# V by seven block products, block columns built in place without the root, and one scores tile, in a one-core attention and FFN layer

## The chip, the cores and the metric

The kernel runs on one core of a Trainium2 chip. The metric is the device time of one execution in microseconds (us). The profile is one execution, taken by the hardware profiler. Its engines are PE (TensorE; PEld is its weight load), DVE (VectorE), ACT (ScalarE), POOL (GpSimd) and SP (SyncE, which here issues DMAs). On-chip memory is SBUF, and TensorE writes its results to PSUM.

## What is computed

One layer of a streaming encoder for 2048 tokens of 1024 features: chunked attention with 16 heads of 64, and then a dense FFN with a width of 2816. Each is preceded and followed by a root-mean-square norm. Cut to what matters:

```
h = rms_norm(x, g_pre_mix)              # x * rsqrt(mean(x^2) + 1e-6) * gain
q, k, v = split_heads(h @ w_qkv)        # 16 heads of 64
for each chunk c of 64 tokens:          # keys: the chunk and the 8 before it
    sc = q[c] @ k[c-8..c] / 8 + bias(head, distance)
    o[c] = softmax(sc) @ v[c-8..c]
x = x + rms_norm(o @ w_o, g_post_mix)
h = rms_norm(x, g_pre_ffn)
x = x + rms_norm((silu(h @ w_gate) * (h @ w_up)) @ w_down, g_post_ffn)
```

A norm is a gain for each feature and one number, the root, for each token. Features lie on the partitions in the products, so the root of a token is a row that multiplies columns, and it can as well be applied to the result of the product.

## The kernel before

**Products.** Each operand is split into hi and lo parts (ACT rounds hi, DVE subtracts it to get lo), and a product is three matmuls, hi·hi, hi·lo and lo·hi (`products`, L184 to L186). Q and K, and gate and up, use seven block products in place of eight for a 2 x 2 block scheme. Their token-side blocks are called B11, B21, T1, T2, B22, T3, T4 and their weight-side blocks A11, A12, S1, S2, S4, S3, A22. T and S blocks are sums and differences of the others. V uses plain products.

**Stages.** `project` takes two groups of 1024 tokens. For each, `values_of` makes V and `queries_keys` makes Q and K (four blocks c of seven products, each in two halves of 12 matmuls), and `emit_v` and `emit_qk` send them to memory. Then attention goes through four quarters n of 512 tokens, eight head pairs p each, and four blocks ib of 128 queries: 128 slots. In a slot stand, in TensorE's order: the scores of a slot two ahead (`scores`, L484 and L485), some products of the quarter's output projection as filler (`o_quarter`), four transposes for each of two heads (L517), more filler, the transposes of the fifth key block (L528), and at each fourth slot the product with V (`output`). Quarter 0 has no fifth block. After a last output projection the FFN runs as gate/up 0, down 0, gate/up 1, down 1 (`gate_up`, `down`).

**What sets the order.** TensorE runs in the order in which the program is written. The other engines' orders are made by a scheduler from the dependences. Side work (the squares and roots of a norm, building blocks, late writes of the residual) stands in a list `later`; `tick` takes its steps as TensorE's work advances, where 1.0 stands for three 512-column matmuls. Weights come through `Stream`, where two numbers of each item say how many items ahead it is loaded and split: (4, 3) before. `block_items` makes the S blocks with four POOL sums (L810).

**Columns before.** For V, `column` multiplies x by the gain, splits it and sums its squares. For Q and K, x is loaded a second time, `norm` multiplies by gain and root (`Blocks.first`, `second`, `third`), and `emit_qk` splits the result straight from PSUM or from its terms (L425, L426). A root takes a sum over partitions on TensorE into a PSUM tile (`pssq`), a power on POOL (L274), and a spread back over partitions by TensorE (`prs`, L334). The program's name for scores in PSUM is `st`, for exponentials in SBUF `sc`, for transposed ones `pT`.

## Time and profile before

| | us |
|---|---|
| time, median of 3 runs | 2571.29 (2569.76 to 2573.14) |
| the profiled execution's own time | 2576.7 |
| its span, first to last instruction | 2574.6 |
| PE busy | 2405.3 (93%), 11562 matmuls |
| DVE busy | 1715.4 (67%) |
| ACT busy | 1156.4 (45%) |
| POOL busy | 648.8 (25%) |

Busy time says which engine is near its limit on the average. Which wait costs time is read by stage and from the waits: a wait row names the instruction that waited, what released it, the total, the number of waits and the mean. Matmuls are pipelined, so that the distance of their starts is what one costs, and not its own duration. `<-` stands between what is written and what is read, and the matmul rows name the tiles by the program's names.

### The profile page before, as it was taken

Reading aid. Unit: us, or ns where it says so; the run is one execution under the profiler, and the core shown is the slowest. Engines: PE = TensorE matmul, PEld = TensorE weight load, DVE = VectorE, ACT = ScalarE, POOL = GpSimd, SP = SyncE. Lnnn points to the kernel's source line nnn. Section 1 sums busy time; section 2 is a strip of 40 time slices with the busy share of each in tenths; the row PEclk is TensorE's granted clock in tenths of the full one; section 3 lists DMA queues with packets and bytes.
Section 4 is the critical chain, followed back from the end, with each engine's and each line's share of the span. In section 5 each row is a group of like instructions: output and inputs, shape, how many; then the busy total and the mean of one; then the engine's idle time right before and its main releaser. Section 6 shows DMA issues by size and latency. Waiting matters only on the chain. (4 is left out here: it accounts for less than half of the span.)

```text
span 2574.6 us, 33484 instructions
## 1 busy us (share of the span) xinstructions
PE 2405.3 (93%) x11562; PEld 1942.4 (75%) x11562; DVE 1715.4 (67%) x2679; ACT 1156.4 (45%) x2047; POOL 648.8 (25%) x501
## 2 busy tenths in 40 slices
PE   8899889977899899998799999999999989999998
PEld 6788677765677676776677888888878878888887
DVE  7767755636565655667877886676768786565567
ACT  5534443326566555565423333345533323334444
POOL 3232124403333433433332232200013222220002
PEclk8999899988899999999899999999999999999999
DMA  7556789859876887885545433356764643336654
GB/s 257 174 152 192 239 251 252 249 156 222 237 208 177 226 237 201 246 241 169 187 144 192 138 102 111 107 184 219 251 203 135 203 160 110 115 104 230 201 181 159
DMA packets 230648, 484.13 MB, mean 188 GB/s; under 512 B 26416, under 2 KB 42816, under 8 KB 227408
## 3 DMA queue, kind: packets, MB, share of 16 engines
q1 hardware_dynamic: 228368, 470.47, 58.9%
q0 software_dynamic: 2112, 11.54, 2.4%
q8 instruction: 91, 1.49, 0.2%
q14 instruction: 77, 0.63, 0.1%
HBM read 370.18 MB, written 134.79 MB: 196 GB/s over the span
## 5 line engine op out<-in xcount | busy, mean ns | idle before, releaser
L810 POOL TENSOR_TENSOR raw<-raw,raw 128x1024 f32<-128x1024 f32 x120 | 318.8, 2656 | 1001.0 <-DVE w_w_T L131 328.0
L184 PE MATMUL pb<-hb,w_w_T 128*128 128x512 f32 x720 | 287.6, 400 | 33.3 <-DVE terms L890 17.5
L501 POOL TENSOR_SCALAR sc<-sc,rows 128x640 f32<-128x640 f32 (+4 forms) x256 | 193.5, 762 | 382.7 <-DVE rows L500 328.8
L186 PE MATMUL pb<-hb,w_w_T 128*128 128x512 f32 x720 | 285.8, 397 | 0.0
L185 PE MATMUL pb<-hb,w_w_T 128*128 128x512 f32 x720 | 285.6, 397 | 0.0
L497 ACT ACTIVATE sc<-sc,nmax 128x640 f32<-128x640 f32 (+4 forms) x256 | 193.1, 756 | 147.1 <-DVE nmax L493 146.9
L493 DVE CUSTOM_DVE_ANT_0 sc<-st,bias 128x640 f32<-128x640 f32 (+4 forms) x256 | 180.4, 738 | 114.6 <-PE st L485 66.2
L184 PE MATMUL pa<-hb,w_w_B 128*128 128x512 f32 x480 | 189.2, 394 | 5.2 <-ACT terms L871 4.5
L184 PEld LDWEIGHTS pb<-hb,w_w_T 128*128 128x128 f32 x720 | 138.8, 193 | 66.9 <-issue 23.6
L185 PE MATMUL pa<-hb,w_w_B 128*128 128x512 f32 x480 | 188.6, 393 | 0.0
L186 PE MATMUL pa<-hb,w_w_B 128*128 128x512 f32 x480 | 188.2, 392 | 0.0
L484 PE MATMUL st<-k,q 128*128 128x384 f32 (+1 forms) x448 | 146.3, 346 | 38.2 <-DVE nmax L493 24.4
L131 DVE TENSOR_TENSOR w_w_T<-raw,w_w_T 128x1024 fp32r<-128x1024 f32 x120 | 163.4, 1362 | 22.5 <-ACT w_w_T L130 21.9
L131 DVE TENSOR_TENSOR w_w_B<-raw,w_w_B 128x1024 fp32r<-128x1024 f32 x90 | 116.1, 1290 | 89.0 <-ACT w_w_B L130 88.9
L130 ACT ACTIVATE w_w_T<-raw 128x1024 fp32r<-128x1024 f32 x120 | 126.7, 1056 | 98.1 <-PE pa L186 43.7
L185 PEld LDWEIGHTS pb<-hb,w_w_T 128*128 128x128 f32 x720 | 139.1, 193 | 28.9
L186 PEld LDWEIGHTS pb<-hb,w_w_T 128*128 128x128 f32 x720 | 138.4, 192 | 29.6
L130 ACT ACTIVATE w_w_B<-raw 128x1024 fp32r<-128x1024 f32 x90 | 95.2, 1058 | 125.2 <-PE pb L186 82.3
L186 PE MATMUL pd<-a,w_d_T 128*128 128x512 f32 (+1 forms) x368 | 139.9, 380 | 0.1
L184 PE MATMUL pd<-a,w_d_T 128*128 128x512 f32 (+1 forms) x368 | 139.9, 380 | 0.0
L185 PE MATMUL pd<-a,w_d_T 128*128 128x512 f32 (+1 forms) x368 | 139.8, 380 | 0.0
L892 ACT ACTIVATE terms<-terms 128x512 f32<-128x512 f32 x65 | 41.1, 632 | 210.5 <-DVE terms L890 210.5
(212 smaller groups left out, 5874.5 us busy)
## 6 DMA issues: line engine op xcount, KB each, us to landing
raw<-in_w_gu SPq DMA_DIRECT2D x88, 512.0 KB, 4.1
q<-q SPq DMA_DIRECT2D x64, 512.0 KB, 6.6
k<-k SPq DMA_DIRECT2D x56, 512.0 KB, 8.6
raw_d<-d_S SPq DMA_DIRECT2D x88, 256.0 KB, 3.5
raw_a<-aT SPq DMA_DIRECT2D x88, 256.0 KB, 3.8
bias<-ext_d SPq DMA_DIRECT2D x128, 144.0 KB, 8.6
aT<-T SPq DMA_DIRECT2D x66, 256.0 KB, 3.1
raw_d<-in_w_d SPq DMA_DIRECT2D x66, 256.0 KB, 3.8
```

The source lines that it names most:

```text
L130: act.activation(hi, raw, AF.Copy)
L131: dve.tensor_tensor(lo, raw, hi.bitcast(F32), op=ALU.subtract)
L184: pe.matmul(pt, a_hi, b_hi, start=first, stop=False, skip_group_check=go_on)
L185: pe.matmul(pt, a_hi, b_lo, start=False, stop=False, skip_group_check=go_on)
L186: pe.matmul(pt, a_lo, b_hi, start=False, stop=last, skip_group_check=go_on)
L484: pe.matmul(st[:, a:b], q[:, 2 * h, cols], kk[:, h, key], start=True, stop=False)
L493: dve.tensor_tensor_reduce(out=sc[:, :n], in0=st[:, c0 : c0 + n], in1=rev, scale=-1.0, scalar=3.0e38, op0=ALU.add, op1=ALU.min, accum_out= ...
L497: act.activation(sc[:, :n], sc[:, :n], AF.Exp, bias=nmax, scale=-1.0, accum_out=rows[:, 0:1])
L501: last_pool[0] = pool.tensor_scalar(sc[:, :n], sc[:, :n], rows[:, 1:2], 1.0, op0=ALU.mult, op1=ALU.mult)
L810: last_pool[0] = pool.tensor_tensor(r[to], r[a], r[b], op=ALU.add)
L892: act.activation(terms[0], terms[0], AF.Silu)
```

## The change

- V is made by the same seven block products (`values_of` is rewritten, w_v is laid out in blocks); the terms are combined by DVE and POOL, and ACT multiplies by the token's root when V leaves.
- x is loaded once, raw, into the slots of T3 and T4. `build` multiplies it there by the gain (ACT), sums the squares (on POOL now), and makes the blocks in place. No root is applied. In Q and K, `emit_qk` multiplies by the row of roots on the way out, on DVE for the results of block B21 and on POOL for the others, and then splits the product `t`.
- The S blocks are summed in place of their raw blocks, so eight raw buffers in project and six in the FFN do; Q, K, gate and up items are loaded six ahead. V needs S blocks too.
- Scores go to one PSUM tile that is kept (`scores_bank`). Its last 256 columns take the fifth-block transposes, which had PSUM tiles of their own. Head 0's scores are cut after 512 columns, and so lie at 0 to 640, and head 1's at 640 to 1280.
- One reciprocal for both heads of a slot, after both maxima; POOL normalises both after it. The first attention job is loaded during the last block of Q and K, into slots of blocks.
- For the FFN's first group only B11, B21 and T1 are built during the last output projection, and the other four blocks during gate/up 0. Both late writes stand in gate/up 0 with wider steps.

```diff
-    def emit_v(n, m, u, pt, ready_):
...
+    def emit_v(n, m, u, t):
+        act.activation(t, t, AF.Copy, scale=rs[n][:, m : m + 1])
+        sp.dma_start(v_d[n][:, m, u * HALF : u * HALF + HALF], t)
+    def emit_qk(n, p, which, src, eng=dve):
         scale = (0.125, 1.0)[which]
+        t = narrow("t")
+        eng.tensor_tensor(t, src, rows_of[n], op=ALU.mult)
         hi, lo = (narrow(m).bitcast(F32R) for m in ("hi", "lo"))
-        act.activation(hi, src, AF.Copy, scale=scale)
-        dve.scalar_tensor_tensor(lo, src, scale, hi.bitcast(F32), op0=ALU.mult, op1=ALU.subtract)
+        act.activation(hi, t, AF.Copy, scale=scale)
+        dve.scalar_tensor_tensor(lo, t, scale, hi.bitcast(F32), op0=ALU.mult, op1=ALU.subtract)
...
+    def scores_bank():
+        if "S" not in phase:
+            phase["S"] = phase["psa"].tile([P, 3 * HALF], F32, name="st", bufs=1)
+        return phase["S"]
...
-                cuts = [(P, 512, 768), (768, 1024, 1408)]
+                cuts = [(0, 512, 640), (640, 1024, 1280)]
...
-            st = phase["psa"].tile([P, 3 * HALF], F32, tag="S", name="st", bufs=1)
+            st = scores_bank()
...
-                dve.reciprocal(rows[:, 1:2], rows[:, 0:1])
...
+            dve.reciprocal(rows[:, 2:4], rows[:, 0:2])
+            for h in range(2):
+                sc = self.sc[ib, h]
+                last_pool[0] = pool.tensor_scalar(
+                    sc[:, :n], sc[:, :n], rows[:, 2 + h : 3 + h], 1.0, op0=ALU.mult, op1=ALU.mult
...
-                tt = phase["psa"].tile([P, 4, P], F32, tag="tt", name="tt", bufs=2)
+                tt = scores_bank()[:, 1280:1536].rearrange("p (h q) -> p h q", h=2)
                 for h in range(2):
                     pe.transpose(tt[:, h, :], sc[h][:, b * P : b * P + P], ident)
-                act.activation(self.pT[:, :, 4, cols], tt[:, 0:2, :], AF.Copy)
+                act.activation(self.pT[:, :, 4, cols], tt, AF.Copy)
...
-    def v_stream(u, k):
...
+            if n == ("B11" if early else "B21"):
+                sum_("A21", "A21", "A22")
+                sum_("A11", "A11", "A21")
             if n == "B21":
...
+                sum_("A12", "A12", "A11")
+            if n == "T2":
+                sum_("A21", "A11", "A22", ALU.subtract)
             return w
...
-            (lambda n=n: fetch_(at.get(n, ())), lambda _, n=n: make(n), 4, 3) for n in BLOCKS
+            (lambda n=n: fetch_(at.get(n, ())), lambda _, n=n: make(n), *ahead.get(n, (6, 3))) for n in BLOCKS
...
+        def after(name, m, pt):
+            if name == "B11":
+                act.activation(p1[m], pt, AF.Copy)
+            elif name == "B21":
+                put(s0, m, 0, pt, p1[m])
+            elif name == "T1":
+                act.activation(z[m], pt, AF.Copy)
+            elif name == "T2":
+                dve.tensor_tensor(p1[m], p1[m], pt, op=ALU.subtract)
+                pool.tensor_tensor(z[m], z[m], p1[m], op=ALU.add)
+            elif name == "B22":
+                put(s1, m, 0, pt, z[m])
+            elif name == "T3":
+                dve.tensor_tensor(p1[m], pt, p1[m], op=ALU.subtract)
+                put(s1, m, 1, pt, z[m], ALU.subtract)
+            else:
+                put(s0, m, 1, pt, p1[m])
...
             def closing(pts, terms, n, p, op=ALU.subtract):
                 def go(i):
                     dve.tensor_tensor(terms[i], pts[i], terms[i], op=op)
-                    emit_qk(n, p, i, terms[i])
+                    emit_qk(n, p, i, terms[i], pool)
...
+            def prep(t, k, x_):
...
+                add_square(x_, totals[2 * g + t], k == 0, pool)
+                act.activation(x_, x_, AF.Copy, scale=gt[:, PRE_MIX, k : k + 1])
...
+                if g + 1 == NG:
+                    if name == "T1":
+                        jobs[0].load(True)
+                    return
...
+                elif name == "T4":
+                    later.extend(timed(
+                        (12.0, roots(2, 3.0)), (15.0, roots(3, 3.0)),
+                        (20.0, build(1, "B22", 3.0)), (34.0, build(1, "T4", 3.0)), (50.0, build(1, "T3", 2.0)),
+                    ))
```

Line numbers in the profile are those of the kernel before. In the orders of the change: L497 and L498 are the scores, L532 the four transposes, L543 the fifth-block transposes and L544 their copy, L418 the product with the row of roots, L421 the lo split, L1201 the subtraction ahead of it, L816 the weight sums, L252 the square sums, L685 and L686 the block differences on POOL, L276 the power of the root.

The first place is TensorE's order within an attention slot, with the waits. First as it was:

```order
L517 MATMUL tt<-ident,sc 128x128 [waits Activation_49,Pool_49]
L517 MATMUL tt<-ident,sc 128x128 x3
L184 MATMUL mm<-hb_24_4549,w_1_6364 128x512
L185 MATMUL mm<-hb_24_4549,w_1_6364 128x512
L186 MATMUL mm<-hb_24_4549,w_1_6364 128x512
L528 MATMUL tt<-ident,sc 128x128 [waits DVE_49]
L528 MATMUL tt<-ident,sc 128x128
L484 MATMUL st<-k_0_7012,q_0_7009 128x384
L485 MATMUL st<-k_0_7012,q_0_7009 128x384
L484 MATMUL st<-k_0_7012,q_0_7009 128x256
L485 MATMUL st<-k_0_7012,q_0_7009 128x256
```

The same place in the change:

```order
L532 MATMUL tt<-ident,sc 128x128 [waits PE_49,Pool_49]
L532 MATMUL tt<-ident,sc 128x128 x3
L184 MATMUL mm<-hb_21_4255,w_0_5534 128x512
L185 MATMUL mm<-hb_21_4255,w_0_5534 128x512
L186 MATMUL mm<-hb_21_4255,w_0_5534 128x512
L543 MATMUL st<-ident,sc 128x128 [waits DVE_49]
L543 MATMUL st<-ident,sc 128x128
L497 MATMUL st<-k_4_5689,q_4_5688 128x512 [waits Activation_49]
L498 MATMUL st<-k_4_5689,q_4_5688 128x512
L497 MATMUL st<-k_4_5689,q_4_5688 128x128
L498 MATMUL st<-k_4_5689,q_4_5688 128x128
```

The fifth-block transposes now write `st`, and the first matmul of the scores waits for ACT. In all 93 slots of quarters 1 to 3 where that matmul waits so, the ACT instruction is the copy L544 of the transposes just ahead of it. The cut of the scores has moved from 384 to 512 columns.

The second place is VectorE's order in Q and K, around the last two blocks of one c (T3 and T4). First as it was:

```order
L1156 TENSOR_TENSOR terms<-pb,terms 128x512
L426 SCALAR_TENSOR_TENSOR lo<-terms,hi 128x512
L1156 TENSOR_TENSOR terms<-pb,terms 128x512
L131 TENSOR_TENSOR w_w_T_1640<-raw_1595,w_w_T_1640 128x1024
L426 SCALAR_TENSOR_TENSOR lo<-terms,hi 128x512
L1156 TENSOR_TENSOR terms<-pb,terms 128x512
L426 SCALAR_TENSOR_TENSOR lo<-terms,hi 128x512
```

and in the change:

```order
L1201 TENSOR_TENSOR terms<-pb,terms 128x512
L421 SCALAR_TENSOR_TENSOR lo<-t,hi 128x512
L1201 TENSOR_TENSOR terms<-pb,terms 128x512
L131 TENSOR_TENSOR w_w_T_1471<-raw_1308,w_w_T_1471 128x1024
L421 SCALAR_TENSOR_TENSOR lo<-t,hi 128x512
L1201 TENSOR_TENSOR terms<-pb,terms 128x512
L421 SCALAR_TENSOR_TENSOR lo<-t,hi 128x512
```

VectorE's order is the same, but the split now reads `t`, which POOL makes from `terms`.

The third place is POOL's order in the change, behind the last Q and K of the first group, up to the powers that give the second group's roots (L276):

```order
L816 TENSOR_TENSOR raw_1852<-raw_1852,raw_1815 128x1024
L686 TENSOR_TENSOR hb_10_1849<-hb_11_1899,hb_10_1849 128x512 x2
L252 TENSOR_TENSOR total<-total,sq 128x512 x2
L685 TENSOR_TENSOR hb_10_1849<-hb_10_1849,hb_11_1899 128x512
L816 TENSOR_TENSOR raw_1902<-raw_1902,raw_1817 128x1024
L685 TENSOR_TENSOR hb_10_1849<-hb_10_1849,hb_11_1899 128x512
L686 TENSOR_TENSOR hb_10_1849<-hb_11_1899,hb_10_1849 128x512 x2
L276 TENSOR_TENSOR hr<-ms,neg_half 128x4
L816 TENSOR_TENSOR raw_1935<-raw_1815,raw_1937 128x1024
L816 TENSOR_TENSOR raw_1994<-raw_1817,raw_1996 128x1024
L276 TENSOR_TENSOR hr<-ms,neg_half 128x4
```

The roots now stand behind weight sums, square sums and block differences. Before, the same two powers stood behind weight sums alone, the square sums having been made by VectorE.

More of the change, by code (lines that the diff above doesn't have):

```diff
@@ L666, in all, with need @@
+        def need(self, name):
+            while name not in self.done:
+                later.popleft()[1]()
         def all(self, w):
@@ L847, in product @@
         def product(pts, name, first, after):
+            if b.raw:
+                b.need(name)
             hi, lo = back.take()
@@ L1101, in columns @@
-    def columns(w, n, cols, total, eng):
-        c = {}
-        def load(k):
-            c[k] = io("x")
-            sp.dma_start(c[k], x[n][:, k, :])
-        return behind(w, KT, 2, load, lambda k: column(n, k, c.pop(k), total, cols, eng))
-    def values_of(n, cols, between):
-        for u in range(2):
-            pts = [bank("pv") for _ in range(4)]
-            for k in range(KT):
-                hi, lo = front.take()
-                for m in range(4):
-                    c = slice(m * P, m * P + P)
-                    products(pts[m], cols.hi(k, c), cols.lo(k, c), hi, lo, k == 0, k == KT - 1)
-                    yield 3 * C512
-                    if k == KT - 1:
-                        emit_v(n, m, u, pts[m], n in said_rs)
@@ L1201, in project @@
[L1201 to L1219 removed]
+        totals = {}
@@ new lines, in now, with roots, go @@
+        def now(steps):
+            for _, f in steps:
+                f()
+        def roots(n, w):
+            def go():
+                later.extendleft(reversed(scaled(n, totals[n], w)))
+            return [(0.0, go)]
+        front.ahead(-8)
+        now(build(0, "L11 each"))
+        for n in (-7, -6, -5):
+            front.ahead(n)
+        now(build(0, "L21"))
+        front.ahead(-4)
+        now(build(0, "L12"))
+        front.ahead(-3)
+        now(build(0, "L22"))
+        for k, (_, f) in enumerate(build(0, "B11")):
+            f()
+            if k == 0:
+                front.ahead(-2)
@@ L1402, in trunk @@
     drain()
[L1403 removed]
+    later.extend(timed(
+        (0.5, first("T2", 3.0)), (13.0, first("B22", 2.0)), (22.0, first("T4", 2.0)), (31.0, first("T3", 1.0)),
+    ))
     for c in ffn():
```

386 lines of the change are left out of this document (214 added, 172 removed).

## The prediction

> **What bounds the kernel now.** I read the stage table first (busy time of each engine by stretch), then the waits of TensorE, then the timeline of single attention slots. In the rows of the stage table the columns are: stretch, its length in us, busy time of PE, PEld, DVE, ACT and POOL with counts, granted PE clock, DMA share, GB/s. The stretches are, in order: V of the first 1024 tokens, Q and K of them, V and then Q and K of the second, attention of quarter 0, of quarters 1 to 3, the last output projection, gate/up 0, down 0, gate/up 1.
>
> ```profile
> 5.90:121.30 115.40, 99.47 (x408) 79.69 (x409) 90.32 (x116) 62.76 (x107) 37.91 (x21) 0.91 0.63 213
> 121.30:282.10 160.80, 154.58 (x674) 127.58 (x674) 116.61 (x129) 74.80 (x111) 36.48 (x15) 0.98 0.61 184
> 282.10:389.30 107.20, 95.66 (x410) 77.29 (x409) 68.34 (x97) 45.70 (x76) 29.12 (x24) 0.94 0.78 245
> 389.30:559.20 169.90, 159.68 (x673) 129.96 (x671) 94.53 (x100) 55.90 (x78) 60.03 (x49) 0.96 0.78 222
> 572.50:676.00 103.50, 79.37 (x444) 60.48 (x445) 62.86 (x248) 60.73 (x180) 37.47 (x69) 0.87 0.96 233
> 676.00:1190.00 514.00, 480.57 (x3061) 364.35 (x3061) 310.51 (x759) 313.06 (x680) 180.15 (x207) 0.99 0.76 212
> 1190.00:1255.00 65.00, 50.54 (x226) 40.00 (x223) 53.79 (x69) 30.61 (x48) 24.29 (x11) 0.89 0.60 201
> 1255.00:1702.00 447.00, 431.18 (x1876) 355.11 (x1876) 316.89 (x362) 149.91 (x202) 111.94 (x45) 0.98 0.42 135
> 1702.00:1912.00 210.00, 210.00 (x928) 173.93 (x928) 147.15 (x229) 111.02 (x193) 0.21 (x1) 1.00 0.72 235
> 1912.00:2349.00 437.00, 425.69 (x1855) 350.76 (x1854) 308.55 (x347) 141.07 (x185) 114.56 (x44) 0.98 0.44 144
> ```
>
> TensorE is the bound nearly everywhere. In down 0 it is busy all 210.00 us for 928 matmuls, so a 512-column matmul costs 210.00/928 = 0.226 us. At that price V of one group (384 matmuls before) would take 86.9 us, and Q and K (672) 152.1. The stages lose 28.5 us (115.4 - 86.9), 8.7, 20.3 and 17.8 to waits and to a clock that falls after them (0.91, 0.94). Quarters 1 to 3 of attention leave 33 of 514 us idle, quarter 0 leaves 24, the last projection 14.5, the two gate/up stages 16 and 11. What TensorE waits for, over the whole span (total us, times, mean):
>
> ```profile
> PE st L484 <- DVE nmax L493: 24.4, 22, 2.1
> PE tt L528 <- DVE pT L520: 18.0, 29, 2.0
> PE pb L184 <- DVE terms L890: 17.5, 6, 5.6
> PE pb L184 <- DVE terms L1156: 15.7, 4, 6.2
> PE pv L185 <- DVE w_v L131: 14.9, 5, 7.0
> PE st L484 <- DMA k<-k: 13.4, 1, 13.4
> PE tt L528 <- ACT pT L522: 7.1, 6, 1.5
> PE prs L334 <- POOL rs L274: 6.5, 3, 4.7
> PE prs L334 <- POOL hr L274: 5.4, 1, 5.4
> ```
>
> **The attention slots: the term that decides.** A slot ends with two fifth-block transposes on TensorE (L528), which ACT copies out of PSUM (L529), and then come the scores of a later slot (L484). Before, these transposes lie in a tile of their own and the scores follow at once:
>
> ```profile
> 899.85 0.44 PE L528 MATMUL tt<-ident,sc 128*128 128x128 f32 x2 [1.35 <-DVE pT L520]
> 900.04 0.42 PE L484 MATMUL st<-k,q 128*128 128x384 f32 x1
> 900.32 0.38 ACT L529 ACTIVATE pT<-tt 128x256 f32<-128x256 f32 x1 [1.14 <-PE tt L528]
> ...
> 908.19 0.44 PE L528 MATMUL tt<-ident,sc 128*128 128x128 f32 x2
> 908.38 0.42 PE L484 MATMUL st<-k,q 128*128 128x384 f32 x1
> 908.46 0.58 ACT L522 ACTIVATE pT<-tt 128x512 f32<-128x512 f32 x1
> 908.94 0.37 ACT L529 ACTIVATE pT<-tt 128x256 f32<-128x256 f32 x1
> ...
> L529 ACT ACTIVATE pT<-tt x96: 361/383/408, 677.5 to 1188.2; 128x256 f32<-128x256 f32 x96
> ```
>
> In the change the transposes go into the last columns of the one scores tile, and the orders shown ahead have the scores wait for an ACT instruction: the copy, whose own input is the matmul just ahead. Nothing lies on TensorE between the transposes and the scores, so TensorE has to stand while ACT copies. At 899.85 the pair ends at 900.29, the copy runs from 900.32 to 900.70, and with 0.06 for the hand-over (an estimate; the other way took 0.03) the scores would start at 900.76, not 900.04: +0.72. At 908.19 ACT is still on an earlier copy, so ours ends at 909.31 and the scores move by +0.99. I did this for all 96 slots of quarters 1 to 3, taking off a wait of the transposes (18.0 and 7.1 us in the rows above) where the later slots would come to ACT when it is idle: the median slot gives 0.83 and the sum is **+80**. Without that credit it is 86. The floor is the shortest copy and short hand-overs, 0.44 + 0.03 + 0.36 + 0.03 - 0.19 = 0.67 a slot, 64 us, with all 25 us of the removed waits taken off: 39. The stall itself is certain by the order; its size lies between.
>
> The scores are also cut otherwise: head 0's 640 columns as 512 + 128 instead of 384 + 256, each twice.
>
> ```profile
> 905.19 0.28 PE L485 MATMUL st<-k,q 128*128 128x256 f32 x1
> 905.31 0.34 PE L484 MATMUL st<-k,q 128*128 128x384 f32 x1
> 905.48 0.34 PE L485 MATMUL st<-k,q 128*128 128x384 f32 x1
> ...
> 606.96 0.27 PE L484 MATMUL st<-k,q 128*128 128x128 f32 x1
> 607.08 0.28 PE L485 MATMUL st<-k,q 128*128 128x128 f32 x1
> ```
>
> Starts lie 0.17 apart after 384 columns, 0.12 after 256 and 0.12 after 128 as well. So 0.226 + 0.12 replaces 0.17 + 0.12: 0.055 twice a slot, 96 slots, **+10**; the wait above does not hide it. The Trainium skill, "TensorE: Matmul & The Clock Gate", section "Back-to-back issue gap", gives an isolated matmul a gap that is proportional to its columns but for 2.5 ns; by it both cuts cost the same and this term would be nothing. The equal 0.12 for 128 and 256 columns speaks against it here. Attention of quarters 1 to 3: +90 (bounds 39 and 96).
>
> **Project.** The prices of what is added and moved:
>
> ```profile
> L1077 POOL TENSOR_TENSOR y<-res,y x16: 1265/1289/1705, 865.3 to 1098.2; 128x512 f32<-128x512 f32 x16
> L426 DVE SCALAR_TENSOR_TENSOR lo<-terms,hi x44: 678/692/2883, 147.4 to 560.6; 128x512 fp32r<-128x512 f32 x44
> L425 ACT ACTIVATE hi<-terms x44: 611/632/636, 146.8 to 560.0; 128x512 fp32r<-128x512 f32 x44
> L1156 DVE TENSOR_TENSOR terms<-pb,terms x28: 676/684/692, 151.6 to 559.2; 128x512 f32<-128x512 f32 x28
> L810 POOL TENSOR_TENSOR raw<-raw,raw x120: 2357/2715/7327, 69.1 to 2302.8; 128x1024 f32<-128x1024 f32 x120
> 420.85 10.36 POOL L810 TENSOR_TENSOR raw<-raw,raw 128x1024 f32<-128x1024 f32 x4 [3.12 <-DMA raw<-in_w_qk]
> 425.38 3.61 DVE L426 SCALAR_TENSOR_TENSOR lo<-terms,hi 128x512 fp32r<-128x512 f32 x2 [5.28 <-DMA q<-hi]
> ```
>
> V loses an eighth of its matmuls: 48 a group, 10.9 us. In the first group the matmuls then need 76.0 us. They start some 9 us later than at 5.9, since a first block needs four columns with square, gain and split on ACT ahead of it (12 ACT operations of about 0.63). The w_v waits (14.9) go, as the weights are asked for six items ahead, and the waits for the two roots (5.4 among them) stay: I put its end at 109 and not 121, **-12**. In the second group POOL has 34 operations ahead of the first root: 14 square sums, 6 products with the root rows and 8 block differences at 1.289, and 6 weight sums at 2.715, 52 us. TensorE asks for that root some 34.5 us after the block behind which this work is queued. It stands about 18, which with a tenth of its time lost otherwise leaves **-1** of the 10.9 won (bounds -15 and +10).
>
> In Q and K the multiply by the root row stands between the subtraction and the split: 0.684 + 1.289 on POOL + 0.632 on ACT + 0.692 = 3.30 us for one half, where TensorE makes a half in 12 x 0.226 = 2.71. DVE's order alternates subtraction and split, so the last block's second subtraction waits for the first one's POOL product. That costs 2 to 5 us in each of 8 blocks, 16 to 40. It takes the place of the four waits of 15.7 us for the same tile; the earlier weights take off most of the remaining 26.5 us that Q and K lose: **-4** (bounds -20 and +30). Project: -17, bounds -40 and +25.
>
> **The rest.** The first attention job's loads are asked for some 60 matmuls earlier, so the 13.4 us for k fall to the tail of the last split and the copies to memory behind it, 7 us: **-6** (-12 to -3). In quarter 0 one reciprocal for two heads, after both maxima, no longer holds up the second maximum behind an exp of ACT; of the 24 us idle I take **-7** (-10 to -4). The last projection builds three FFN blocks instead of seven, so of its 14.5 us idle 9 go: **-9**. The other four are built under gate/up 0, where DVE has 447 - 317 = 130 us free. The two late writes with wider steps and the earlier weights take perhaps half of the 27 us that both gate/up stages lose (17.5 in the row of terms L890): **-12**. FFN and last projection together: bounds -40 and -5; had these stages no free DVE time, the four blocks would cost their 16 splits, 16 x 0.69 = 11 us.
>
> **Sum**, against the profiled execution of 2576.7 us: +90 - 17 - 6 - 7 - 9 - 12 = +39, 2616. That execution is 5.4 above the median of the runs, 2571.3, so on the scale of the medians **2610**.
>
> **The rivals.**
>
> *R1, POOL's queue and DVE's port make project slower.* Two lo splits took 3.61 us instead of 2 x 0.692 while POOL made four sums in 10.36 (rows above). The change gives POOL 48 products, 16 more weight sums and the square sums, all beside DVE's splits. For: POOL's work in project, 163.5 us before, grows by at least 48 x 1.289 + 16 x 2.715 = 105 us. Against: POOL is then still idle for half of the stage. If every Q and K block loses 5 us and the root stall is 30, project is 35 worse: 2645. The Trainium skill, "SBUF — State Buffer", section "SBUF: two separate sides", says that DVE operations with two SBUF inputs and GpSimd operations take a shared port pair as an exclusive lock for the whole instruction. The 3.61 us agree.
>
> *R2, the other side: the weights asked for earlier end the stalls.* Place: the waits for w_v, terms and weights in project and gate/up. Together those stages lose 28.5 + 8.7 + 20.3 + 17.8 + 16 + 11 = 102 us. If six tenths of these go (61) with the 21.8 us of matmuls, and quarter 0, the boundary and the last projection give their 22, that is -105; with attention at +90 it makes 2556. From -95 on the kernel is faster than before. Against: half of the loss hangs on DVE, ACT and POOL, not on loads.
>
> *R3, the attention wait stays near its floor.* The waits of the transposes go as TensorE comes later: +39 + 10, with the other terms -51: 2569, no change that can be told.
>
> *R4, the wait named in the order is already met when TensorE gets there.* Then attention costs 10 only and the kernel is at 2530. Against: the copy's input is the matmul just ahead, so it can't have run.
>
> **How the numbers follow.** Main case 0.58 (own range 2585 to 2640), R1 0.16, R2 0.13, R3 0.09, R4 0.04. A measurement of this kernel tells about 0.2%, 5 us, from no change. Faster: R2, R4 and a little of R3, 0.18; same 0.07; slower 0.75. The range reaches from R2's 2555 to just past R1's 2645: 2555 to 2650.
>
> **What would show it.** In the profile after: TensorE's scores waiting for ACT's fifth copy, about 90 times, 0.6 to 0.9 us each, and quarters 1 to 3 near 604 us instead of 514; a wait for a root of 15 us or more early in the second V; POOL's products in front of DVE's split in Q and K; V of the first group ending near 109 us. I am wrong if the scores wait less than 0.5 us each, if quarters 1 to 3 stay under 560, or if project shrinks by more than 40.

## The result: 4.2% slower, more than the range allowed

| | us |
|---|---|
| before, median of 4 runs | 2572.22 (2569.76 to 2575.84) |
| changed kernel, median of 4 runs | 2678.62 (2675.12 to 2685.28) |
| ratio | 1.0416, 95% interval 1.0392 to 1.044 |
| forecast | 2610, range 2555 to 2650 |

The direction was right and the size was not: +106 us on the medians, where +39 was forecast. The two profiled spans, 2574.6 and 2673.4 us, differ by 98.8. They can be compared stage by stage, each stage taken from its first matmul to the first matmul of the next (the start of V of the first group moves from 5.9 to 9.0 and is counted with it):

| stage | before | after | measured | forecast |
|---|---|---|---|---|
| V, first group, with its start | 121.3 | 119.3 | -2.0 | -12 |
| Q and K, first group | 160.8 | 202.6 | +41.8 | Q and K of both groups: -4 |
| V, second group | 107.2 | 99.9 | -7.3 | -1 |
| Q and K, second group | 169.9 | 170.7 | +0.8 | (see above) |
| the gap ahead of attention | 13.3 | 0 | -13.3 | -6 |
| attention, quarter 0 | 109.7 | 112.6 | +2.9 | -7 |
| attention, quarters 1 to 3 | 509.9 | 611.9 | +102.0 | +90 |
| last output projection | 63.3 | 55.2 | -8.1 | -9 |
| gate/up 0 and 1 | 883.8 | 861.2 | -22.6 | -12 |
| down 0 and 1 | 435.3 | 439.9 | +4.6 | 0 |

(Small differences from the stretches quoted in the prediction come from where the first matmul lies.) The stage table of the changed kernel, with the same columns as before, for the first V, the first Q and K, the second V, and quarters 1 to 3:

```profile
5.90:119.30 113.40, 93.45 (x361) 72.31 (x362) 90.86 (x80) 67.43 (x105) 79.25 (x40) 0.86 0.38 136
119.30:321.90 202.60, 166.86 (x674) 134.49 (x673) 124.78 (x120) 74.80 (x111) 94.08 (x49) 0.91 0.45 140
321.90:421.80 99.90, 82.28 (x361) 67.44 (x360) 67.46 (x65) 47.16 (x70) 57.46 (x33) 0.90 0.43 132
698.00:1317.60 619.60, 512.18 (x3080) 380.15 (x3078) 314.27 (x666) 311.17 (x682) 179.71 (x207) 0.97 0.62 176
```

The first Q and K has the same 674 matmuls as before, but stands idle for 36 us where it was 6, and the matmuls themselves take 167 and not 155 us, at a granted clock of 0.91 and not 0.98. That clock is a mean of stretches at 1.00 and at 0.50: from 301.4 to 304.7 us and from 308.3 to 321.7 it is 0.50, and there 512-column matmuls start 0.43 us apart, where 0.23 is the distance at 1.00. What TensorE waits for in the changed kernel, over its span (total us, times, and the longest single wait; the text ahead and the prediction called this last column a mean, which it is not):

```profile
PE st L497 <- ACT pT L544: 95.3, 93, 3.3
PE pb L184 <- DVE terms L1201: 31.2, 9, 11.5
PE st L497 <- DVE nmax L506: 20.7, 17, 6.0
PE prs L336 <- POOL hr L276: 18.2, 2, 14.4
PE pa L184 <- ACT terms L1193: 17.1, 6, 5.9
...
PE st L543 <- DVE nmax L506: 7.8, 8, 1.7
...
PE st L497 <- DMA k<-k: 4.4, 2, 2.5
...
PE pv L185 <- DVE w_wv_B L131: 3.2, 1, 3.2
```

The first row is new and is the forecast wait: 93 times, the scores for ACT's copy of the fifth-block transposes. The second and fifth are Q and K. The 13.4 us for k before attention are gone but for 4.4, and the waits of the transposes for the other copies (25 us before) are gone as well. The row of L543 is new too: the fifth-block transposes, which now write the scores' tile, wait 8 times for DVE to have read the scores there.

### The profile page after: what moved, and what is told of

Its sections match the earlier page's. It is cut to its first block, busy times and chain, and to the rows that moved or that the text cites. A ratio compares the mean times of both kernels' runs of the same rounds, so it can differ in the third digit from the quotient of the medians.

```text
span 2673.4 us, 33185 instructions
## 1 busy us (share of the span) xinstructions
PE 2419.3 (90%) x11466; PEld 1938.0 (72%) x11466; DVE 1739.1 (65%) x2470; ACT 1153.4 (43%) x2039; POOL 809.5 (30%) x598
## 5 line engine op out<-in xcount | busy, mean ns | idle before, releaser
L816 POOL TENSOR_TENSOR raw<-raw,raw 128x1024 f32<-128x1024 f32 x136 | 358.9, 2640 | 911.2 <-DMA raw<-in_w_gu 439.6
L506 DVE CUSTOM_DVE_ANT_0 sc<-st,bias 128x640 f32<-128x640 f32 (+2 forms) x248 | 175.9, 746 | 154.1 <-PE st L498 130.7
L497 PE MATMUL st<-k,q 128*128 128x512 f32 (+3 forms) x440 | 153.9, 362 | 113.5 <-ACT pT L544 95.3
L184 PE MATMUL pb<-hb,w_wg_T 128*128 128x512 f32 x528 | 207.3, 393 | 8.0 <-DVE terms L918 7.3
L186 PE MATMUL pb<-hb,w_wg_T 128*128 128x512 f32 x528 | 206.9, 392 | 0.0
L185 PE MATMUL pb<-hb,w_wg_T 128*128 128x512 f32 x528 | 206.6, 391 | 0.0
L497 PEld LDWEIGHTS st<-k,q 128*128 128x128 f32 x440 | 86.7, 197 | 146.0 <-ACT pT L544 117.3
L184 PE MATMUL pa<-hb,w_wg_B 128*128 128x512 f32 x352 | 137.3, 390 | 1.8 <-ACT terms L899 1.8
L186 PE MATMUL pa<-hb,w_wg_B 128*128 128x512 f32 x352 | 137.0, 389 | 0.0
L185 PE MATMUL pa<-hb,w_wg_B 128*128 128x512 f32 x352 | 136.9, 389 | 0.0
L532 PEld LDWEIGHTS tt<-ident,sc 128*128 128x128 f32 x928 | 110.2, 145 | 30.6 <-POOL sc L517 15.4
L498 PE MATMUL st<-k,q 128*128 128x512 f32 (+3 forms) x440 | 132.3, 333 | 0.0
L131 DVE TENSOR_TENSOR w_wg_T<-raw,w_wg_T 128x1024 fp32r<-128x1024 f32 x88 | 123.6, 1405 | 11.6 <-ACT w_wg_T L130 11.5
L559 PE MATMUL po<-pT,v 128*64 128x128 f32 (+3 forms) x864 | 130.6, 451 | 0.0
L532 PE MATMUL tt<-ident,sc 128*128 128x128 f32 x928 | 129.5, 282 | 0.0
L421 DVE SCALAR_TENSOR_TENSOR lo<-t,hi 128x512 fp32r<-128x512 f32 x64 | 72.8, 1137 | 76.8 <-ACT hi L420 76.7
```

What stands on the lines that cost most here:

```text
L131: dve.tensor_tensor(lo, raw, hi.bitcast(F32), op=ALU.subtract)
L184: pe.matmul(pt, a_hi, b_hi, start=first, stop=False, skip_group_check=go_on)
L185: pe.matmul(pt, a_hi, b_lo, start=False, stop=False, skip_group_check=go_on)
L186: pe.matmul(pt, a_lo, b_hi, start=False, stop=last, skip_group_check=go_on)
L497: pe.matmul(st[:, a:b], q[:, 2 * h, cols], kk[:, h, key], start=True, stop=False)
L498: pe.matmul(st[:, a:b], q[:, 2 * h + 1, cols], kk[:, h, key], start=False, stop=True)
```

## The experiments

My theory after the result had two parts. **A:** in quarters 1 to 3 the scores wait for a copy that only the shared tile makes them wait for. **P:** in Q and K the product by the root row is a hop to POOL, where it queues behind weight sums, and the DVE, ACT and POOL queues pass the delay on to TensorE. The rivals: DVE and ACT would hold the attention slots anyway; DVE's order of subtraction and split holds Q and K; or POOL's sums block DVE there whoever makes the product. The last one is the mechanism of the prediction's R1.

The stages that the runs were made for, in us, from first matmul to first matmul. Here the second Q and K has the gap ahead of attention with it (169.9 + 13.3 before).

| kernel | ratio to before (95%) | Q, K first | V second | Q, K second | quarters 1 to 3 |
|---|---|---|---|---|---|
| before | 1 | 160.8 | 107.2 | 183.3 | 509.9 |
| the change | 1.0416 (1.0392 to 1.044) | 202.6 | 99.9 | 170.8 | 611.9 |
| e1 own tile | 1.0055 (1.0039 to 1.0071) | 203.1 | 99.9 | 173.5 | 526.8 |
| e2 own tile, old cuts | 0.9999 (0.9984 to 1.0014) | 200.9 | 99.9 | 170.1 | 513.0 |
| e3 product on DVE | 1.0295 (1.0273 to 1.0318) | 176.4 | 99.7 | 165.8 | 618.8 |
| e4 subtractions first | 1.0396 (1.0378 to 1.0415) | 201.0 | 101.7 | 170.8 | 614.6 |
| e5 before, scores tile | 1.0387 (1.0363 to 1.041) | 160.8 | 109.1 | 185.1 | 607.1 |
| e6 no root product | 1.0218 (1.0198 to 1.0238) | 165.4 | 97.6 | 158.2 | 614.2 |
| e7 no weight sums | 1.0341 (1.0325 to 1.0358) | 187.9 | 99.9 | 164.6 | 614.5 |
| e8 e2 and e3 together | 0.9896 (0.9878 to 0.9915) | 174.6 | 101.9 | 168.0 | 510.2 |
| e9 before, POOL hop | 1.0147 (1.0132 to 1.0162) | 177.9 | 119.1 | 198.3 | 508.5 |
| e10 e8, squares on DVE | 0.9861 (0.9846 to 0.9875) | 178.5 | 92.9 | 167.7 | 509.6 |
| e11 e10, blocks spread | 0.9869 (0.9855 to 0.9884) | 171.3 | 95.6 | 171.3 | 512.9 |
| e12 e8, loads four ahead | 0.9882 (0.9855 to 0.9909) | 176.1 | 101.3 | 168.7 | 511.6 |

### The attention slots

**e1: the transposes in a tile of their own again.**

```diff
-                tt = scores_bank()[:, 1280:1536].rearrange("p (h q) -> p h q", h=2)
+                tt = phase["psa"].tile([P, 4, P], F32, tag="tt", name="tt", bufs=2)
...
-                act.activation(self.pT[:, :, 4, cols], tt, AF.Copy)
+                act.activation(self.pT[:, :, 4, cols], tt[:, 0:2, :], AF.Copy)
```

> The change with one edit undone: the fifth-block transposes get a PSUM tile of their own again. If the wait of the scores for ACT's copy is what costs in quarters 1 to 3 (95 us in 93 waits, and some 15 for the restarts of TensorE behind them), these quarters fall from 619 to about 530 us, with some 25 us of waits for the other copies coming back, and the time from 2679 to about 2590. If TensorE was held there by DVE and ACT anyway, the wait moves to other rows and less than 40 us come back.

The median is 2587.38, 91 us under the change, and quarters 1 to 3 take 526.8 us. The scores no longer wait for ACT. In the waits of this run the old rows are back, and they are about what they were before:

```profile
PE st L497 <- DVE nmax L506: 23.8, 21, 6.0
PE tt L543 <- DVE pT L535: 20.7, 26, 3.1
...
PE tt L543 <- ACT pT L537: 9.4, 8, 2.2
```

So A holds, and the rival (held by DVE and ACT anyway) falls. The first scores go to columns 0 to 512 and the copy reads columns 1280 to 1536, so it is the common tile that orders them and no common data. Whether one tile with a finer wait would do as well was not tried.

**e2: the old cuts as well.**

```diff
-                cuts = [(0, 512, 640), (640, 1024, 1280)]
+                cuts = [(P, 512, 768), (768, 1024, 1408)]
```

> As the run before, with the old cut of head 0's scores (384 + 256) as well. If a matmul of 128 columns costs what one of 256 does, another 11 us go from quarters 1 to 3, and the time is about 2580. If a matmul's price is proportional to its columns, nothing changes against the run before.

Another 13.8 us go (526.8 to 513.0), and the ratio falls from 1.0055 to 0.9999. By the stage, a cut of 512 + 128 columns is dearer than 384 + 256 by some 0.07 us, twice in each of 96 slots. From the first start to the next instruction's start, the eight score matmuls of a slot take 1.40 us on average in e1 and 1.28 in e2, which is 0.06 twice a slot, or 11 of the 13.8 us. The rest of the change, without its attention edits on the tile, comes out even with the kernel before.

**e5: the part alone, in the kernel before.**

```diff
-                cuts = [(P, 512, 768), (768, 1024, 1408)]
+                cuts = [(0, 512, 640), (640, 1024, 1280)]
...
-            st = phase["psa"].tile([P, 3 * HALF], F32, tag="S", name="st", bufs=1)
+            st = scores_bank()
...
-                tt = phase["psa"].tile([P, 4, P], F32, tag="tt", name="tt", bufs=2)
+                tt = scores_bank()[:, 1280:1536].rearrange("p (h q) -> p h q", h=2)
```

> The kernel before with the scores tile alone: fifth-block transposes in its last 256 columns and the new cuts, all else as before. If the scores' wait for ACT's copy is a cost of its own, quarters 1 to 3 go from 510 to about 612 us and the time from 2574 to about 2676. If it costs only together with the change's other edits of attention (the merged reciprocal), less than 60 us.

The median is 2672.22 beside 2571.18, +101, and quarters 1 to 3 take 607.1 us. The wait is the same, with no other edit of the change (the new cuts are part of this run):

```profile
PE st L490 <- ACT pT L535: 92.6, 93, 3.3
```

### Q and K

In one block of the first Q and K of the change, the timeline (start, duration, engine, line, operation; in brackets the idle time and what ended it) shows where a half product's result goes (other rows left out):

```profile
190.70 2.39 POOL L816 TENSOR_TENSOR raw<-raw,raw 128x1024 f32<-128x1024 f32 x1 [18.99 <-DMA raw<-in_w_qk]
190.76 3.42 DVE L131 TENSOR_TENSOR w_w_B<-raw,w_w_B 128x1024 fp32r<-128x1024 f32 x1 [0.46 <-ACT w_w_B L130]
194.10 0.68 DVE L1201 TENSOR_TENSOR terms<-pc,terms 128x512 f32<-128x512 f32 x1
194.25 2.40 POOL L816 TENSOR_TENSOR raw<-raw,raw 128x1024 f32<-128x1024 f32 x1 [1.16 <-DVE w_w_B L131]
196.61 1.30 POOL L418 TENSOR_TENSOR t<-terms,total 128x512 f32<-128x512 f32 x1
197.94 0.63 ACT L420 ACTIVATE hi<-t 128x512 fp32r<-128x512 f32 x1 [7.21 <-POOL t L418]
198.60 0.69 DVE L421 SCALAR_TENSOR_TENSOR lo<-t,hi 128x512 fp32r<-128x512 f32 x1 [3.83 <-ACT hi L420]
199.22 0.68 DVE L1201 TENSOR_TENSOR terms<-pc,terms 128x512 f32<-128x512 f32 x1
199.82 1.22 DVE L131 TENSOR_TENSOR w_w_B<-raw,w_w_B 128x1024 fp32r<-128x1024 f32 x1
199.98 2.17 POOL L418 TENSOR_TENSOR t<-terms,total 128x512 f32<-128x512 f32 x1 [2.07 <-DVE terms L1201]
202.11 2.33 POOL L816 TENSOR_TENSOR raw<-raw,raw 128x1024 f32<-128x1024 f32 x1
202.18 0.63 ACT L420 ACTIVATE hi<-t 128x512 fp32r<-128x512 f32 x1 [2.66 <-POOL t L418]
202.85 2.15 DVE L421 SCALAR_TENSOR_TENSOR lo<-t,hi 128x512 fp32r<-128x512 f32 x1 [1.81 <-ACT hi L420]
204.93 0.68 DVE L1201 TENSOR_TENSOR terms<-pb,terms 128x512 f32<-128x512 f32 x1
205.68 1.27 POOL L418 TENSOR_TENSOR t<-terms,total 128x512 f32<-128x512 f32 x1 [1.23 <-DVE terms L1201]
205.75 0.75 PE L184 MATMUL pb<-hb,w_w_T 128*128 128x512 f32 x1 [5.30 <-DVE terms L1201]
```

The subtraction is done at 194.78. The product waits for POOL's weight sum until 196.61, ACT for the product, DVE's split for ACT, and DVE's next subtraction stands behind that split in DVE's queue. DVE works 9.5 of the 14.9 us from 190.76 to 205.61, and yet the subtraction that TensorE needs comes 5.30 us late. Some operations are also longer beside each other: DVE's weight split takes 3.42 us when it starts just after a POOL sum, and 1.22 when it starts ahead of POOL's product, which then takes 2.17 and not 1.30; the lo split beside the next POOL sum takes 2.15 and not 0.69. The last two add 2.3 us to this chain. Over the stage DVE stands idle 44.6 us ahead of 30 splits. Before, it was 13.3 us ahead of 27, of which 4.9 us ahead of the 19 of subtracted terms:

```profile
L421 DVE SCALAR_TENSOR_TENSOR lo<-t,hi 128x512 fp32r<-128x512 f32 x30 | 34.4, 1146 | 44.6 <-ACT hi L420 44.6
```

```profile
L426 DVE SCALAR_TENSOR_TENSOR lo<-terms,hi 128x512 fp32r<-128x512 f32 x19 | 16.5, 869 | 4.9 <-ACT hi L425 4.9
...
L426 DVE SCALAR_TENSOR_TENSOR lo<-pa,hi 128x512 fp32r<-128x512 f32 x8 | 5.5, 691 | 8.4 <-ACT hi L425 8.4
```

The first fence is the change, the second the kernel before, from the groups of DVE in that stage. TensorE's waits in the first Q and K of the change (119.3 to 321.9 us) are these two rows, 35.7 us in all:

```profile
PE pb L184 <- DVE terms L1201: 26.8, 5, 11.5
PE pa L184 <- ACT terms L1193: 8.9, 3, 3.2
```

Seven of the eight, 24.2 us, stand twice a block: ahead of T4 for DVE's subtraction (5.0, 5.3, 3.1 and 1.8 us), and ahead of the next block's B21 for ACT's copy of B11's result (2.6, 3.1 and 3.2 us). The eighth, 11.5 us, is the second half of the last T4, where DVE, ACT and POOL already build the second group's blocks. Fewer scratch buffers for `t`, hi and lo (7 in project, 9 before) are not what holds the chain: wherever ACT had been idle ahead of `hi` in this stage, `hi` starts within 0.1 us of the end of `t`.

**e3: the product on DVE.**

```diff
-                    emit_qk(n, p, i, terms[i], pool)
+                    emit_qk(n, p, i, terms[i])
```

> The change with the product by the root row made by DVE and not POOL in Q and K. If the hop to POOL and POOL's queue of weight sums ahead of it make the first Q and K stage 42 us longer, that stage falls from 203 to about 165 us and the time to about 2640. If the loss is DVE blocked by POOL's weight and square sums (its splits at 2.2 us where 0.69 was measured before), the stage stays above 185, as DVE gets 48 products more and POOL's sums stay.

The time falls by 30 us to 2648.73, and the first Q and K from 202.6 to 176.4: a gain of 26 us for an edit that gives DVE more work. It stays above the 165 that P alone would give, and below the 185 of the rival, so this run alone decides for neither.

**e4: both subtractions first.**

```diff
                     dve.tensor_tensor(terms[i], pts[i], terms[i], op=op)
-                    emit_qk(n, p, i, terms[i], pool)
+                    if i == 1:
+                        emit_qk(n, p, 0, terms[0], pool)
+                        emit_qk(n, p, 1, terms[1], pool)
```

> The change with the two subtractions of a block written ahead of both products and splits. If DVE's alternation of subtraction and split holds TensorE ahead of T4, the waits for the subtracted terms in Q and K (31 us in 9 waits over the project stage) fall under 12 and the first Q and K stage from 203 to about 180. If POOL's queue holds them, the same wait stands there or at the next block, and the stage changes by under 8 us.

The stage takes 201.0 us, and the ratio (1.0396) has an interval that overlaps the change's. But the run does not test the alternation. Only TensorE's order is that of the program; the others are made by a scheduler, and in the first three blocks c of this stage DVE's subtractions (L1201) and splits (L421) still take turns, as in the change. DVE in the first block, with the weight split left out:

```profile
144.49 0.69 DVE L1201 TENSOR_TENSOR terms<-pc,terms 128x512 f32<-128x512 f32 x1 [0.34 <-PE pc L186]
150.71 0.69 DVE L421 SCALAR_TENSOR_TENSOR lo<-t,hi 128x512 fp32r<-128x512 f32 x1 [5.52 <-ACT hi L420]
151.32 0.68 DVE L1201 TENSOR_TENSOR terms<-pc,terms 128x512 f32<-128x512 f32 x1
...
154.95 2.15 DVE L421 SCALAR_TENSOR_TENSOR lo<-t,hi 128x512 fp32r<-128x512 f32 x1 [1.81 <-ACT hi L420]
157.02 0.68 DVE L1201 TENSOR_TENSOR terms<-pb,terms 128x512 f32<-128x512 f32 x1
```

TensorE's waits ahead of T4 in these blocks are 5.2, 5.2 and 3.1 us, where the change has 5.0, 5.3 and 3.1. What an order with both subtractions first would give stays open. The waits in this run, from 119 to 330 us:

```profile
PE pb L184 <- DVE terms L1201: 22.8, 5, 5.7
PE pa L184 <- ACT terms L1193: 8.4, 3, 3.3
```

**e6: no product at all, in Q and K's subtracted results.**

```diff
-        t = narrow("t")
-        eng.tensor_tensor(t, src, rows_of[n], op=ALU.mult)
+        t = src
+        if eng is dve:
+            t = narrow("t")
+            eng.tensor_tensor(t, src, rows_of[n], op=ALU.mult)
```

> The change without the 48 POOL products by the root row in Q and K (this leaves the root out of those results). It shows the price of the step itself. If the hop is the whole cause, the first Q and K stage falls from 203 to about 161 us as before. If POOL's sums beside DVE have a part of their own, it stays near 175, where the product on DVE left it.

The first Q and K takes 165.4 us, 37 of the 42 less, and the second one 12.6 less. The product is nearly the whole cause; beside it POOL's sums have little of their own there. TensorE's waits in the stage, from 120.1 to 285.5 us:

```profile
PE pb L184 <- DVE terms L1203: 9.6, 2, 9.4
```

Both stand at the end of the stage, so the long wait there (11.5 us in the change) is mostly not the product's. In the first three blocks there is no wait, though DVE's order of subtraction and split is the same as in the change: the alternation without the product holds nothing up.

**e7: no weight sums in Q and K, the product kept on POOL.**

```diff
         def sum_(to, a, b, op=ALU.add):
+            if ahead is None or early and len(key) == 2 and key[0] in "01":
+                return
```

> The change without the 32 POOL weight sums of Q and K (their S blocks are left unsummed), the products by the root row still on POOL. If the products cost because they queue behind sums of 2.4 us each on POOL, and DVE is blocked beside these, the first Q and K stage falls from 203 to about 175 us. If the hop costs by its own length (3.3 us a half against 2.7), it stays above 190.

The stage takes 187.9 us, between the two cases. With e6: 14.7 us of the product's 37 need the weight sums ahead of it and beside DVE, and the other 22.5 (187.9 - 165.4) stay without them. How much of the 14.7 is queueing on POOL and how much DVE held up beside POOL's sums, this run can't separate; nor how much of the 22.5 is DVE and POOL holding each other up at the product itself and at the square sums, which stay.

**e9: the hop alone, in the kernel before.** The POOL operation doubles the terms, and the split halves its scale.

```diff
-    def emit_qk(n, p, which, src):
+    def emit_qk(n, p, which, src, hop=False):
         scale = (0.125, 1.0)[which]
+        if hop:
+            t = io("t")
+            pool.tensor_tensor(t, src, src, op=ALU.add)
+            src, scale = t, 0.5 * scale
...
-                    emit_qk(n, p, i, terms[i])
+                    emit_qk(n, p, i, terms[i], True)
```

> The kernel before with a POOL operation of the same size ahead of the split of the 48 subtracted terms of Q and K (it doubles them, and the split halves its scale), and nothing else of the change. If the hop through POOL is enough to hold TensorE, the first Q and K stage goes from 161 us to 180 or more and the time up by 25 to 50 us. If it needs the change's other POOL work in project (square sums, V's weight sums), these stages stay within 10 us.

The median is 2613.77 beside 2574.8, +39: 17 us in the first Q and K, 15 in the second, and 12 in the second V. Its waits, the answer of the trace to 575 us (15.7 in 4 waits for the same subtraction before):

```profile
PE pb L184 <- DVE terms L1160: 31.9, 7, 9.2
...
PE pa L184 <- ACT terms L1152: 9.7, 5, 4.2
```

The `t` of this run lies in three buffers that from 250 us on also hold the second group's x columns, so the end of the first stage and the second V are no clean measure of the hop. Ahead of 250 us, TensorE waits 9.2 us in 5 waits in the first Q and K, where before it had no wait there. So the hop costs without any other edit of the change, and P holds in this form: the hop first, the sums ahead of it second.

### What beats both kernels, and what stays

**e8: e2 and e3 together.**

> The change with a tile of its own for the fifth-block transposes, the old cuts and the product by the root row on DVE. If the terms found so far simply add (91, 14 and 30 us), the time is 2679 - 135 = 2544, some 30 below the kernel before. If they overlap, it is near 2574.

The median is 2544.08 beside 2571.18, a ratio of 0.9896. The terms add: to within a microsecond of the sum of the single runs by the medians, and to within 5 by the ratios. The change's other parts are worth some 27 us, once the scores have their own tile and POOL does not stand between a subtraction and its split.

**e10: the second group's square sums on DVE.**

```diff
-                add_square(x_, totals[2 * g + t], k == 0, pool)
+                add_square(x_, totals[2 * g + t], k == 0, dve if g else pool)
```

> The fastest kernel so far (2544 us) with the second group's square sums on DVE and not POOL. If POOL's queue ahead of the first root is what TensorE waits for in the second V (11 to 14 us in one wait), that wait falls under 5 us and the time to about 2535. If DVE is then the late one, the time stays within 5 us of 2544.

The second V goes from 101.9 to 92.9 us, as the root comes earlier, though its longest wait is still 6.4. In its place the end of the first Q and K waits 14.7 us for ACT's hi part of a block:

```profile
PE pb L184 <- ACT hb L340: 14.7, 1, 14.7
...
PE prs L336 <- POOL hr L276: 10.2, 2, 6.4
```

The whole gains little: 3 us by the medians (2540.71), 9 by the ratios, whose intervals (0.9846 to 0.9875, and 0.9878 to 0.9915 for e8) just don't touch. It has the lowest median of the kernels.

**e11: the same, with the blocks of the second group built over a longer time** (T1 behind the last block of Q and K, T2 and the second root during V):

```diff
-                elif name == "T2":
...
                 elif name == "B22":
-                    later.extend(timed((0.5, build(1, "T1", 1.8))))
-                elif name == "T3":
-                    later.extend(timed((0.5, build(1, "T2", 3.0))))
+                    later.extend(timed((0.5, build(1, "B21", 1.8))))
                 elif name == "T4":
                     later.extend(timed(
-                        (12.0, roots(2, 3.0)), (15.0, roots(3, 3.0)),
-                        (20.0, build(1, "B22", 3.0)), (34.0, build(1, "T4", 3.0)), (50.0, build(1, "T3", 2.0)),
+                        (0.5, build(1, "T1", 2.0)), (12.0, roots(2, 3.0)), (14.0, build(1, "T2", 3.0)),
+                        (28.0, roots(3, 3.0)), (32.0, build(1, "B22", 3.0)), (46.0, build(1, "T4", 3.0)),
+                        (58.0, build(1, "T3", 2.0)),
```

> As the run before, with the second group's block building spread: T1 behind the last Q and K, T2 under V. If the 10.6 us wait at the end of the first Q and K stage is DVE, ACT and POOL loaded with this building, it goes and the time is some 10 us lower than the run before. If the blocks then come too late for V, the second V stage gets it back.

The first Q and K falls by 7 us, the second V and the second Q and K give them back (2.7 and 3.6), and the ratio is e10's within its interval. The 14.7 us wait is gone; spreading moves it, and does not save it.

**e12: gate/up weights four ahead again, in e8.**

```diff
-        items.extend(i for c in range(NC) for i in block_items(w_gu[c], f"g{g}{c}"))
+        items.extend(i for c in range(NC) for i in block_items(w_gu[c], f"g{g}{c}", True, {n: (4, 3) for n in BLOCKS}))
```

> The fastest kernel so far (2544 us) with the gate/up weights asked for four items ahead again and not six. If the earlier weights are what took 12 us off gate/up 0 and 10 off gate/up 1, these stages go back to about 447 and 437 us and the time to 2565. If the wider steps of the side work did it, they stay at 434 and 427.

Gate/up 0 and 1 take 433.0 and 426.7 us, as in the change. So the earlier loads are not what made these stages 22.6 us shorter. Which of the other edits does it (the wider steps of side work, fewer blocks built, or the weight sums spread over three items) was not tried.

## Why the prediction was wrong

**Quarters 1 to 3, +90, measured +102: right in the mechanism, and near in size.** The wait is where the order put it, 93 times. The slot-by-slot sum gave 80 for it, and undoing it alone gives 85.1 (611.9 - 526.8). The cuts were 13.8 by the stage and not 10, and 3.1 us are left between e2 and the kernel before: 102.0 together. Waits by themselves rise from 27 to 104 us. A slot loses more than its wait row shows, since the pair of transposes has to end before the copy, which the sum had in it. Below, the scores start 1.21 us after the pair starts (699.84 - 698.63), with a wait of 0.83; at 899.85 in the kernel before it was 0.19 without a wait.

```profile
698.63 0.38 PE L543 MATMUL st<-ident,sc 128*128 128x128 f32 x2
699.41 0.38 ACT L544 ACTIVATE pT<-st 128x256 f32<-128x256 f32 x1
699.84 0.50 PE L497 MATMUL st<-k,q 128*128 128x512 f32 x1 [0.83 <-ACT pT L544]
700.17 0.39 PE L498 MATMUL st<-k,q 128*128 128x512 f32 x1
```

(Other engines' rows are left out.) A slow restart, for which e1's expectation has some 15 us, adds little: the first of a slot's scores leads the next by 0.34 us on average here, and by 0.32 in e1, where it does not wait; that is 2 us for 93.

The formula for an isolated matmul in the Trainium skill, "TensorE: Matmul & The Clock Gate", section "Back-to-back issue gap", by which the cuts would cost the same, is not borne out here: 13.8 us lie between e1 and e2, whose only difference they are. The Trainium skill itself says in that section that the formula counts too little for few columns.

**Q and K, -4, measured +42.6: the step that failed.** The prediction priced the chain of one half at 3.30 us beside TensorE's 2.71, took 16 to 40 us for it, and then set against it the old waits for the same tile (15.7 us) and most of the other losses, which earlier weights were to take off. Both terms of this sum were mis-sized:

- The product costs 49.8 us in the two groups (202.6 - 165.4 and 170.8 - 158.2, e6), where the middle of 16 to 40 is 28. The chain is longer than the sum of its operations. POOL had a sum of 2.4 us ahead of the product, the product itself took up to 2.17 us where 1.289 was the row, the lo split up to 2.15 where 0.692 was, and DVE and ACT pass the delay on, being held in order behind the split. In the first group 15 of the product's 37 us need the weight sums (e7), and a product on DVE costs 11 of the 37 (e3 beside e6).
- The credit was 32 us, if the product's cost is taken as 28. But Q and K lost 26.5 us in all, and the 15.7 are part of these, so the sum took off more than was there. Without the product the two groups are only some 7 us shorter than before, the gap ahead of attention apart: +4.6 and -11.7 (e6). The 50 of the product less these 7 make the 42.6.
- No price was set on the clock, which is a part of the above. At 0.91 the same 674 matmuls of the first group took 12.3 us more.

This was rival R1, with a chance of 0.16 and 2645 as its time. Its place was right. Its Q and K price, 5 us in every block, was near the 42.6 in 8 blocks; its root stall of 30 us was 14.4. Project came out 50 us above the forecast, where R1 had 35 and the upper end of the range left 40 for everything, and the attention term was 12 above at the same time. The Trainium skill, "SBUF — State Buffer", section "SBUF: two separate sides", describes DVE and GpSimd operations that block one another for a whole instruction. The trace agrees: DVE's weight split took 3.42 us beside a POOL sum and 1.22 ahead of POOL's product. How large a part of the 37 us this is was not separated: without any weight sum 22.5 us stay, and the products and square sums on POOL stay with them.

**V, -12 and -1, measured -2.0 and -7.3: together near enough, apart not.** In the first group the matmuls became fewer, but those left ran at a granted clock of 0.86: 93.45 us for 361, 0.259 each, where 0.244 was before and 0.226 is the full pace. The start came 3.1 us later and not 9. The sum had 76.0 us of matmuls at full pace and left some 18 us for the rest; from its first matmul the stage takes 110.3, so that 34 were lost. In the second group the root's wait came nearly as forecast (14.4 us for 18; the other 3.8 us of the L276 row are the first group's root), and the other losses went below what was assumed.

**The gap ahead of attention, -6, measured -13.3,** and quarter 0, -7, measured +2.9: the tail of the last split, which the sum had kept in the gap, stands as a wait of 6.0 us at the second slot of quarter 0 (the longest of the nmax row). Together -10.4 for -13.

**Last projection and FFN, -21, measured -26:** right in sum; the reason given for gate/up (earlier weights) fell with e12.

**The rivals.** R2 (stalls in project and gate/up dissolve) did not happen in project; the waits for V's weights fell from 14.9 to 3.2 us, but the hop took more. R3 (attention near its floor of 39 us) falls: the waits of the transposes did go, 25 us, and yet the wait is 95. R4 (the wait already met) falls with 93 waits of 1.0 us.

## What to carry to other kernels

Before a step is put between a result and the engine that frees its place, count what stands ahead of it on its new engine and what stands behind it on the old one: in-order queues turn a 1.3 us product on a half-idle engine into 37 us over a stage, while the same product on a busier engine cost 11. A PSUM tile that two kinds of work shared made the scores wait for the transposes' reader in 93 of 96 slots, and the transposes for the scores' reader in 8; a tile of its own was worth 85 us here. Check a credit against the loss that is there: a stage that loses 26.5 us can't give back 32. And look in the trace whether an edit of the program's order reached the engine: in e4 it did not.

## What was not expected of the hardware

A score matmul of 128 columns took about as much of TensorE's time as one of 256: the new cuts cost 13.8 us for 192 pairs of matmuls, 0.07 each, of which 0.06 lie within the scores. The first score matmul of a slot leads the next by some 0.1 us more than its neighbours do, whether it waited (0.34 us) or not (0.32 us in e1). Over a stage with waits in each block the same matmuls took 8% longer (166.86 beside 154.58 us) at a granted clock of 0.91, which is a mean: the matmuls start 0.23 us apart in stretches at 1.00 and 0.43 us apart in stretches at 0.50.

```profile
316.67 0.80 PE L184 MATMUL pb<-hb,w_w_T 128*128 128x512 f32 x1 [11.50 <-DVE terms L1201]
317.26 0.63 PE L185 MATMUL pb<-hb,w_w_T 128*128 128x512 f32 x1
317.69 0.63 PE L186 MATMUL pb<-hb,w_w_T 128*128 128x512 f32 x1
318.11 0.63 PE L184 MATMUL pb<-hb,w_w_T 128*128 128x512 f32 x1
```
